# RMSNorm with SiLU on one core: block 0 loaded as two partition halves, one from each hardware queue

## The chip, the cores and the metric

The kernel runs on one core of a Trainium2 chip. The metric is device time in microseconds (us) of one execution. "Ratio" is always the mean time of one kernel's fast runs over the mean of the other kernel's fast runs of the same rounds on the same chip; it is therefore not exactly the ratio of the medians that stand beside it.

## The reference

```python
# x: 8 x 1024 x 2048 float32, gamma: 2048 float32, eps = 1e-5
rms = np.sqrt(np.mean(x ** 2, axis=-1, keepdims=True) + eps)
out = gamma * x / rms
return out * (1 / (1 + np.exp(-out)))
```

That is 8192 independent rows of 8 KB. 67.1 MB are read and 67.1 MB are written.

## The kernel before

The rows are cut into 16 blocks of 4 MB. A block is one tile of 128 partitions, and each partition holds 4 rows next to each other (32 KB). Six buffers go round. Loads are issued by SyncE (SP), stores and gamma by ScalarE (ACT).

```python
J = 4; BUFS, LEAD = 6, 6; nblk = n // (P * J)          # P = 128, nblk = 16
xb = x2.rearrange("(b p j) d -> b p (j d)", p=P, j=J)
...
def load(b):
    xt = pool.tile([P, J * d], f32, name="xt")
    nc.sync.dma_start(out=xt, in_=xb[b])
    blocks[b] = xt
...
def sums(b, after_first=()):
    ...   # sums of squares: two rows per partition on VectorE, two on ScalarE
    ...   # after ScalarE's first square: store(s) for the blocks in after_first
def store(b):
    nc.scalar.dma_start(out=ob[b], in_=blocks[b])
    if b + LEAD < nblk:
        load(b + LEAD)                                  # into the buffer just stored
...
grow = pool.tile([P, J * d], f32, name="xt")            # the sixth buffer takes gamma first
for b in range(BUFS - 1):
    load(b)
...
nc.scalar.dma_start(out=grow[0:P:P // Q, 0:w], in_=...) # gamma, 8 KB
...                                                     # TensorE spreads gamma over partitions
nc.vector.tensor_copy(out=g, in_=junk_v)                # stands before the first sums on VectorE
load(BUFS - 1)
...
for b in range(1, last - 1):
    sums(b + 1, after_first=[b - 1])
    finish(b)                                           # x * rstd * gamma, then SiLU
    invert(b + 1)
```

## Time and profile before

| | before |
|---|---|
| median time | 317.37 us (317.27 to 317.58), 3 runs |
| busy share of VectorE / ScalarE | 71% / 71% |
| load queue q1 plus store queue q10, share of 16 transfer engines | 98.9% |
| block 0 usable / first store issued | 13.2 us / 36.67 us |

The prediction below quotes the slice rows and the opening of this profile. Two more views of it matter later. The first is the page's row of rates, GB/s in 40 slices of 7.9 us:

```profile
GB/s 328 402 464 410 452 390 410 452 419 443 439 424 452 411 452 410 452 414 456 406 456 414 448 414 448 439 423 452 414 452 410 452 414 456 406 456 410 452 407 269
```

From the second slice to the last but one, the rate stands near 430 (390 to 464). The second view is busy time by stretches. Its last two columns are the share of the transfer engines (DMA) and GB/s. Both count a packet (here one partition's 32 KB), with all its time and bytes, in the stretch in which it starts, so a share can pass 1.

```profile
4.00:20.00 16.00, 2.09 (x8) 0.55 (x8) 7.28 (x7) 5.91 (x7) 0.00 (x0) 1.00 0.99 429
20.00:24.00 4.00, 0.00 (x0) 0.00 (x0) 4.00 (x2) 0.96 (x1) 0.00 (x0) 1.00 0.93 401
```

At 4 to 20 us a DMA share of 0.99 goes with 429 GB/s. A share and a rate say different things: the share says how long packets were in flight, the rate how much they carried. In this kernel they go together. Keep that pair for the comparison.

### The profile page before, as it was taken

The numbers are of one execution on the slowest core, as the hardware profiler recorded it, in microseconds if no ns is written. First come the engines' busy times: TensorE is split into PE (matmuls) and PEld (weight loads), VectorE is DVE, ScalarE is ACT, GpSimd is POOL, SyncE is SP. The second block draws the span as 40 slices with busy tenths as digits, with TensorE's granted clock in tenths as the row PEclk, the third lists the DMA queues.
The fourth block names the chain that finished last, engine by engine and source line by source line (L and its number), as shares of the span: only waits on it lengthen the run. The fifth ranks groups of instructions, "written<-read, shape, count | busy, mean of one in ns | idle before, by whom it ended". The sixth has DMA issues, their size and how long they took to land.

```text
span 316.3 us, 444 instructions
## 1 busy us (share of the span) xinstructions
PE 2.1 (1%) x8; PEld 0.5 (0%) x8; DVE 223.5 (71%) x147; ACT 223.8 (71%) x144; POOL 0.2 (0%) x4
## 2 busy tenths in 40 slices
PE   0200000000000000000000000000000000000000
PEld 0000000000000000000000000000000000000000
DVE  0679499999493983939849397593966939993900
ACT  1357958999967777678676687676786776879540
POOL 0000000000000000000000000000000000000000
DMA  8999999999999999999999999999999999999996
GB/s 328 402 464 410 452 390 410 452 419 443 439 424 452 411 452 410 452 414 456 406 456 414 448 414 448 439 423 452 414 452 410 452 414 456 406 456 410 452 407 269
DMA packets 4763, 134.25 MB, mean 425 GB/s; under 512 B 532, under 2 KB 532, under 8 KB 536
## 3 DMA queue, kind: packets, MB, share of 16 engines
q1 hardware_dynamic: 2304, 67.11, 49.7%
q10 hardware_dynamic: 2456, 67.12, 49.2%
q14 instruction: 3, 0.02, 0.0%
HBM read 67.12 MB, written 67.11 MB: 424 GB/s over the span
## 4 chain that ended last, share of the span: by engine, by line
DMA 74%; DVE 14%; ACT 5%; issue 2%; DVEq 1%; ACTq 0%; SPq 0%
DMA xt<-in_x_dram 44%; DMA out_dram<-xt 30%; DVE xt L84 11%; ACT xt L88 3%; DVE junk_v L64 3%; ACT junk_a L68 1%; DVEq L164 1%; ACT L74 0%; ACT rms L74 0%; DVE rstd L79 0%; ACTq L93 0%; DVE ss L64 0%; SPq L52 0%; DVEq L64 0%; ACTq L74 0%
## 5 line engine op out<-in xcount | busy, mean ns | idle before, releaser
L84 DVE SCALAR_TENSOR_TENSOR xt<-xt,rstd,g 128x2048 f32<-128x2048 f32 x64 | 146.2, 2347 | 0.1
L88 ACT ACTIVATE xt<-xt 128x4096 f32<-128x4096 f32 x32 | 115.4, 3615 | 36.8 <-DVE xt L84 36.7
L64 DVE CUSTOM_DVE_ANT_0 junk_v<-xt 128x2048 f32<-128x2048 f32 x32 | 73.5, 2298 | 56.1 <-DMA xt<-in_x_dram 55.5
L68 ACT ACTIVATE junk_a<-xt 128x2048 f32<-128x2048 f32 x32 | 60.1, 1879 | 29.2 <-DMA xt<-in_x_dram 28.3
L74 ACT ACT_TABLE_LOAD x15 | 19.2, 1283 | 9.9 <-DVE ss L64 9.9
L88 ACT ACT_TABLE_LOAD x15 | 19.2, 1283 | 3.1 <-DVE xt L84 2.9
L79 DVE RECIPROCAL rstd<-rms 128x4 f32<-128x4 f32 x16 | 2.8, 172 | 11.3 <-ACT rms L74 11.3
L114 DVE COPY g<-junk_v 128x2048 f32<-128x2048 f32 x1 | 2.3, 2292 | 9.2 <-PE junk_v L112 9.2
L68 ACT ACTIVATION_READ_ACCUMULATOR junk_a<-xt 128x1 f32 x32 | 6.0, 186 | 0.0
L74 ACT ACTIVATE rms<-ss,eps_t 128x4 f32<-128x4 f32 x16 | 4.8, 297 | 1.2 <-DVE ss L64 1.1
L64 DVE DVE_READ_ACCUMULATOR2_ANT ss<- 128x1 f32 x32 | 4.5, 141 | 0.0
L112 PE MATMUL junk_v<-xt,ones 1*128 1x512 f32 x8 | 2.1, 1133 | 8.1 <-DMA xt<-in_gamma_dram 8.1
L107 ACT ACT_TABLE_LOAD x1 | 1.3, 1283 | 0.7 <-PEq L150 0.7
L105 DVE MEMSET ones<- 128x128 f32 x1 | 0.2, 165 | 0.8 <-PEq L150 0.8
L112 PEld LDWEIGHTS junk_v<-xt,ones 1*128 1x128 f32 x8 | 0.5, 306 | 8.1 <-issue 8.1
L107 ACT ACTIVATE junk_a<-ones 128x1 f32<-128x1 f32 x1 | 0.2, 174 | 0.0
L150 POOL MEMSET const-uint8-127<- 128x1 uint8 x1 | 0.1, 102 | 0.0
L150 POOL MEMSET const-bfloat16-1.0<- 128x1 bf16 x1 | 0.1, 101 | 0.0
L150 POOL MEMSET const-float32-0.0<- 128x1 f32 x1 | 0.1, 98 | 0.2 <-issue 0.2
L150 POOL MEMSET const-float32-1.0<- 128x1 f32 x1 | 0.1, 98 | 0.0
L106 DVE MEMSET eps_t<- 128x1 f32 x1 | 0.1, 59 | 0.0
## 6 DMA issues: line engine op xcount, KB each, us to landing
xt<-in_x_dram SPq DMA_DIRECT2D x16, 4096.0 KB, 42.0
out_dram<-xt ACTq DMA_DIRECT2D x15, 4096.0 KB, 35.2
out_dram<-xt ACTq DMA_DIRECT2D x2, 2048.0 KB, 10.4
xt<-in_gamma_dram ACTq DMA_DIRECT2D x1, 8.0 KB
```

The costliest lines, as they stand in the source:

```text
L64: nc.vector.tensor_tensor_reduce(out=junk_v, in0=row(b, j), in1=row(b, j), scale=1.0, scalar=0.0, op0=ALU.mult, op1=ALU.add, accum_out=ss[ ...
L68: nc.scalar.activation(out=junk_a, in_=row(b, j), func=ACT.Square, accum_out=ss[:, j:j + 1])
L74: nc.scalar.activation(out=rms, in_=ss, func=ACT.Sqrt, scale=1.0 / d, bias=eps_t)
L79: nc.vector.reciprocal(out=rstd, in_=rmss.pop(b))
L84: nc.vector.scalar_tensor_tensor(out=row(b, j), in0=row(b, j), scalar=rstds[b][:, j:j + 1], in1=g, op0=ALU.mult, op1=ALU.mult)
L88: nc.scalar.activation(out=blocks[b][:, cols], in_=blocks[b][:, cols], func=ACT.Silu)
L105: nc.vector.memset(ones, 1.0)
L107: nc.scalar.activation(out=junk_a[:, 0:1], in_=ones[:, 0:1], func=ACT.Square)
L112: nc.tensor.matmul(junk_v[:, c * w:(c + 1) * w], ones[k:k + 1, :], grow[k:k + 1, 0:w], start=True, stop=True)
L114: nc.vector.tensor_copy(out=g, in_=junk_v)
L150: nc = _bacc.Bacc("TRN2", target_bir_lowering=False, num_devices=1)
L164: with _tile.TileContext(nc) as tc:
```

## The change

The intent is to have both hardware queues fetch block 0 at the start, where ScalarE's queue has nothing else to do. Here is the diff without an empty line:

```diff
     def load(b):
         xt = pool.tile([P, J * d], f32, name="xt")
-        nc.sync.dma_start(out=xt, in_=xb[b])
+        if b == 0:
+            nc.sync.dma_start(out=xt[0:P // 2, :], in_=xb[b][0:P // 2])
+            nc.scalar.dma_start(out=xt[P // 2:P, :], in_=xb[b][P // 2:P])
+        else:
+            nc.sync.dma_start(out=xt, in_=xb[b])
         blocks[b] = xt
```

## The prediction

> **What bounds the kernel now.** I read the page's slice rows and its queue table first[...]:
>
> ```profile
> DVE  0679499999493983939849397593966939993900
> ACT  1357958999967777678676687676786776879540
> DMA  8999999999999999999999999999999999999996
> ...
> q1 hardware_dynamic: 2304, 67.11, 49.7%
> q10 hardware_dynamic: 2456, 67.12, 49.2%
> ```
>
> The transfer engines are busy in all 40 slices, VectorE (DVE) and ScalarE (ACT) only 71% of the span each. q1 carries the loads, q10 the stores and gamma; together they fill 98.9% of 16 engines' time. 134.25 MB in 316.3 us is 424 GB/s. To see that this holds in each stage I asked for busy time in stretches; the last two columns are the share of the transfer engines and GB/s:
>
> ```profile
> 0.00:2.00 2.00, 0.00 (x0) 0.00 (x0) 0.17 (x2) 1.27 (x1) 0.20 (x4) 1.00 0.71 180
> 2.00:4.00 2.00, 0.00 (x0) 0.00 (x0) 0.00 (x0) 0.18 (x2) 0.00 (x0) 1.00 0.81 311
> ...
> 50.00:100.00 50.00, 0.00 (x0) 0.00 (x0) 43.40 (x29) 45.22 (x29) 0.00 (x0) 1.00 1.00 431
> 100.00:200.00 100.00, 0.00 (x0) 0.00 (x0) 69.00 (x45) 71.92 (x46) 0.00 (x0) 1.00 1.01 435
> ```
>
> From 4 us to the end nothing is idle. The list of who waited for whom agrees: VectorE's longest wait is for loads (55.5 us in 11 waits), and the store queue is never empty after the first store: a 4 MB store takes 35.2 us from issue to landing, where 4.19 MB at 431 GB/s is 9.7 us. So time lost by the transfer engines adds to the end, and time lost by VectorE or ScalarE doesn't, up to a slack. At the tail that slack is the last half store: issued at 304.77 us, landing after about 10.4 us, though 2.1 MB at 431 GB/s needs 4.9; some 5 us of other stores lay ahead of it. The opening, in order of time:
>
> ```profile
> 0.73 9.82 SPq L52 DMA_DIRECT2D xt<-in_x_dram  x6
> ...
> 1.03 1.09 ACTq L108 DMA_DIRECT2D xt<-in_gamma_dram  x1
> ...
> 8.09 2.09 PE L112 MATMUL junk_v<-xt,ones 1*128 1x512 f32 x8 [8.09 <-DMA xt<-in_gamma_dram]
> 10.24 2.29 DVE L114 COPY g<-junk_v 128x2048 f32<-128x2048 f32 x1 [9.24 <-PE junk_v L112]
> 13.19 1.88 ACT L68 ACTIVATE junk_a<-xt 128x2048 f32<-128x2048 f32 x1 [10.99 <-DMA xt<-in_x_dram]
> 13.24 2.30 DVE L64 CUSTOM_DVE_ANT_0 junk_v<-xt 128x2048 f32<-128x2048 f32 x1 [0.71 <-DMA xt<-in_x_dram]
> ```
>
> Block 0 lands at 13.1 us, and the copy of gamma is finished 0.7 us earlier. In the trace's packet records block 0 is eight 32 KB packets on each of 16 engines; the first took 1.55 to 2.28 us, the rest 1.21 to 1.23. I call 1.22 us a round. Gamma's four 2 KB packets, issued by 2.12 us, started only at 6.12, after three rounds of block 0, and their semaphore writes came one round later.
>
> [...] No run yet shows halves; that one queue alone fills the engines is shown (431 GB/s from 4.19 MB in 9.7 us, eight rounds of 1.22). [...] The trace agrees with a delay: gamma entered behind three committed packets. The first store agrees too: 24.75 us from issue to landing is about 8 own + 8 load + 4 committed rounds, 20 x 1.22 = 24.4. [...]
>
> **The change part by part.**
>
> *Removed and added.* SyncE's first 4 MB issue becomes a 2 MB issue, ScalarE gets a 2 MB issue ahead of its first table load. ScalarE's own cost is one issue, 0.34 (stores) to 1.09 us (gamma), while it waits 10.99 us for block 0 anyway: nothing. Bytes are the same; 16 more semaphore packets of 9 ns: nothing. SyncE's issues took 0.33 to 0.51 us each and are far ahead of the data: nothing.
>
> *Moved: block 0.* Half A (q1) and half B (q10) together are the same eight rounds, but q1 goes straight on with block 1. If B enters behind three committed packets, as gamma did, an engine's order is A A A B A B L B L B (L is block 1), and B ends in round 10 instead of 8. That is 2 x 1.22 = 2.4 us later: block 0 usable at 15.5, or 16.7 if its semaphore write waits another round. If both halves alternate from the start it stays at 13.1.
>
> *Moved: gamma.* It is now behind B on q10. Data at about 16, semaphore a round later (17.4), 0.45 us to PE as before: 17.9. Then 2.1 us PE and 2.3 us copy: VectorE reaches its first sum at 22.4 instead of 13.24, some 9 us late (6.5 if the halves alternate). VectorE is nearly solid from 28.96 to 79.5, so the first stores go out 6.5 to 9 us late, from 36.67 to 43 or 46.
>
> *Does that lateness reach the end?* The six loads need 48 rounds, until about 61 us, alone. A store issued at 46 meets 12 rounds of loads still to go; the other queue covers every gap, and store 1 (55.8 + 9 = 65) is out before store 0 lands (46 + 24.4 = 70). VectorE needs 4 x 2.35 + 2 x 2.30 + about 0.5 = 14.5 us per block against 19.5 of transfer (8.4 MB at 431), so it gains 5 us per block once loads pace it; it already waits 4.46 us at 84.1 and 5.54 at 103.5. Gone by block 7. Worth 0 on the end.
>
> [...] Four A packets and four B packets on each engine, all doubled because the engines run nearly in step (starts in a round spread over 0.6 us), cost 8 x 1.22 = 9.8 us. If engines fall out of step after the first three A packets [...], it is 3 x 1.22 = 3.7 us. The transfer engines have no idle time to give this back: it adds to the end, 321 to 327 us. Gamma and block 0 would come up to 12 us later still (first stores near 57 us), and by the same counting the queues only just stay fed; I allow 1 us for that.
>
> The sum: 317.4 + 0 (issues) + 0 (late gamma) + 0, 3.7 or 9.8 (ports) = 317.4, 321.1 or 327.2.
>
> **The rivals.** *It is hidden:* the engines are the limit and any order of the same packets ends together: 317.4. For it: mixed loads and stores also give 1.22 us a packet per engine, so the engine itself is a limit. [...] *Faster start:* two queues fill sooner. The first 4 us moved 0.98 MB, where 431 GB/s gives 1.72; that is 1.7 us lost, mostly the wait before 1.73 us and the first packet's 0.8 us of extra latency. Perhaps 0.3 us of it could be saved, so over 2% (6.3 us) faster is not to be had. *VectorE becomes the bound at the start:* the lateness above; it costs only if both queues run dry, which I counted against.
>
> **Range and chances.** [...] No effect is 30%, at 317.4 within 0.5. The distribution has two heaps; its middle is about 322. The range from 317.0 to 328.5 takes in both. Faster by over 2%: 2%, for a misread opening. Within 2%: 52%. Slower: 46%.
>
> **What would show it.** [...] rates in the first 25 us well under 431 (200 to 300 GB/s), first sums of block 0 at 20 to 30 us, and after 40 us the same 431 to 435 as before. Right for the hidden version: 431 GB/s from 4 us on, block 0's squares at 13 to 17 us, the gamma matmul at 15 to 18, first store at 43 to 46, and the same end. The step "lateness is worth 0" is wrong if a stretch after 40 us moves clearly less than 431 GB/s. The prediction is wrong altogether if a half uses fewer engines than 16, if the tail's 5 us slack is used up, or if the order of stores and loads changes for the rest of the run.

The 3.7 and 9.8 us that its sum calls ports were my estimate of what is lost if a packet of a half takes two rounds of 1.22 us instead of one, for three packets or for all eight; the trace of the kernel before has no load of half the partitions, and so shows no such packet. I gave some such effect 70%, and 46% to one above the 6.35 us that make 2%. That half a block is still spread over 16 engines was assumed too. Packets it calls committed are those that went ahead of a later issue: three rounds before gamma. That the queues take turns is in the packet records of the kernel before: the first store was issued at 36.67 us, its first packet started at 40.8, and from 44 to 57 us rounds of load and store packets alternate.

## The result, and the profile after

| | before | after |
|---|---|---|
| median time, 6 runs each | 317.48 us (317.27 to 317.81) | 326.60 us (326.38 to 326.76) |
| ratio | | 1.0287 (95%: 1.0274 to 1.0300) |
| span of the profiled run | 316.3 us | 324.9 us |

The change makes the kernel 9.1 us slower. The rows of the page after, and its queue table:

```profile
DVE  0004794999999999939397593957949399939100
ACT  1004369589999999996786676686676677795400
DMA  8999999999999999999999999999999999999996
GB/s 194 202 254 449 452 399 440 452 416 424 452 432 412 446 448 412 432 448 420 432 444 444 416 432 448 420 428 444 448 412 436 444 420 432 440 448 417 432 422 297
...
q10 hardware_dynamic: 2536, 69.22, 50.9%
q1 hardware_dynamic: 2240, 65.01, 48.0%
```

The DMA row is the same, digit for digit, as before. The GB/s row isn't: the first three of its slices (8.1 us each) carry a little over half of what they did. The stretches show the same:

```profile
4.00:20.00 16.00, 0.00 (x0) 0.00 (x0) 0.00 (x0) 0.00 (x0) 0.00 (x0) 1.00 1.07 229
20.00:24.00 4.00, 0.00 (x0) 0.00 (x0) 0.00 (x0) 0.00 (x0) 0.00 (x0) 1.00 0.74 262
24.00:50.00 26.00, 2.09 (x8) 0.55 (x8) 19.64 (x13) 13.80 (x9) 0.00 (x0) 1.00 1.00 429
50.00:100.00 50.00, 0.00 (x0) 0.00 (x0) 45.31 (x33) 44.92 (x33) 0.00 (x0) 1.00 1.01 438
100.00:200.00 100.00, 0.00 (x0) 0.00 (x0) 79.77 (x52) 85.28 (x55) 0.00 (x0) 1.00 1.00 430
```

From 4 to 20 us the transfer engines are as busy as before (1.07 against 0.99) but move 229 GB/s instead of 429. From 24 us on the rates are those of the kernel before. So the loss is one event, at the load of block 0. The packet records agree: counted at equal bytes moved, the changed kernel is 9.1 us behind at 4.5 MB and 8.7 to 10.0 us behind from 9 MB to the end, with no further loss.

The opening in order of time:

```profile
0.73 0.54 SPq L53 DMA_DIRECT2D xt<-in_x_dram  x1
0.73 0.58 ACTq L54 DMA_DIRECT2D xt<-in_x_dram  x1
...
1.41 1.14 ACTq L113 DMA_DIRECT2D xt<-in_gamma_dram  x1
...
24.13 1.88 ACT L72 ACTIVATE junk_a<-xt 128x2048 f32<-128x2048 f32 x1 [21.32 <-DMA xt<-in_x_dram]
...
26.37 2.09 PE L117 MATMUL junk_v<-xt,ones 1*128 1x512 f32 x8 [26.37 <-DMA xt<-in_gamma_dram]
...
28.52 2.29 DVE L119 COPY g<-junk_v 128x2048 f32<-128x2048 f32 x1 [27.52 <-PE junk_v L117]
30.85 2.30 DVE L68 CUSTOM_DVE_ANT_0 junk_v<-xt 128x2048 f32<-128x2048 f32 x1
```

Block 0 becomes usable at 24.13 instead of 13.19 us. Gamma follows on the store queue, and VectorE's first sum starts at 30.85 instead of 13.24 us. The first store goes out at 54.27 us, 17.6 later than before.

The packet records of the two traces give the size. Block 0 is 128 packets of 32 KB, eight on each of 16 engines (the records name the queue and not the engine; the rounds are read from the start times, which fall into eight groups of 16). All packets of block 0, the slow first round included, took 1.31 us on average before and 2.41 after: 8 x (2.41 - 1.31) = 8.8 us. The first packets of block 1 start at 12.40 us on average before and at 21.62 after, 9.2 us later: the 8.8, and 0.46 us by which the very first packets started later (2.38 us on average instead of 1.92). That is, within noise, the 9.1 us of the result (8.6 between the spans of the two profiled runs, of which the one before was slower than its median). The engines went through the rounds in step, in the order A A B A B A B B (A is the half of SyncE's queue, B the other): in each round all 16 packets are of the same half.

One view misleads here, the chain that ended last, by engine:

```profile
DMA 30%; ACT 19%; DVE 18%; another core or an unknown queue 18%; issue 7%; DVEq 1%; PE 1%; SPq 0%; ACTq 0%
```

Before, this chain was 74% DMA. Now it runs back through VectorE and ScalarE to the late gamma. Taken at its word it says that compute, and gamma, hold the end. Whether that is so is one of the questions for the experiments.

### The profile page after: what moved, and what is told of

It reads as the page before. It is cut to its first block, busy times and chain, and to the rows that moved or that the text cites. A ratio compares the mean times of both kernels' runs of the same rounds, so it can differ in the third digit from the quotient of the medians.

```text
span 324.9 us, 445 instructions
## 1 busy us (share of the span) xinstructions
PE 2.1 (1%) x8; PEld 0.5 (0%) x8; DVE 223.2 (69%) x147; ACT 223.2 (69%) x144; POOL 0.2 (0%) x4
## 4 chain that ended last, share of the span: by engine, by line
DMA 30%; ACT 19%; DVE 18%; another core or an unknown queue 18%; issue 7%; DVEq 1%; PE 1%; SPq 0%; ACTq 0%
DMA out_dram<-xt 14%; DVE xt L88 13%; ACT xt L92 13%; DMA xt<-in_x_dram 8%; DMA xt<-in_gamma_dram 8%; DVE junk_v L68 4%; ACT junk_a L72 2%; ACT L78 2%; ACT L92 2%; DVE g L119 1%; DVEq L169 1%; PE junk_v L117 1%; ACT rms L78 1%; SPq L56 0%
```

## The experiments

My theory: the packets of a transfer that covers only a contiguous range of the partitions slow each other, so that each takes two rounds instead of one. What slows them is shown by no run; that a packet takes two rounds in quarters and four in eighths, as the expectations below have it, was my estimate. In most of the expectations the first figure is the theory's and the last a rival's. The rivals are that two queues taking turns cost the time, that each cut of a transfer costs, that the order in which HBM is read costs, or that the late gamma and the late first store cost. Eleven kernels were run. All gave the right result except the two that are marked. Median of the kernel before: 317.86 us for same_queue, all_ports, late_gamma and mid_block, 317.57 for quarters, eighths, even_odd and store_halves, 317.64 for the other three.

### Both halves on one queue: same_queue

```diff
-            nc.scalar.dma_start(out=xt[P // 2:P, :], in_=xb[b][P // 2:P])
+            nc.sync.dma_start(out=xt[P // 2:P, :], in_=xb[b][P // 2:P])
```

> Both halves of block 0 go out on the load queue, none on the store queue. [...] 326.6 us as in the changed kernel, +9.1 over before; block 0's packets still about 2.4 us each, squares of block 0 at 22 to 24 us, gamma early again (PE at 8 to 12 us). Rival, that two queues taking turns on the load side cost the time: 317.5 us, packets 1.22 us each.

Measured: 327.40 us, ratio 1.0299 (1.0283 to 1.0314). The packets of block 0 took 2.53 us on average. The first square started at 23.97 us, gamma reached TensorE at 13.39. The second queue isn't the cause. VectorE's first sum started at 24.03 us, 6.8 us sooner than in the changed kernel, and the time was no better: a first hint that compute's lateness isn't what costs.

### The same halves of HBM spread over all partitions: all_ports

```diff
+        if b == 0:
+            src = x2[0:P * J].rearrange("(h p j) d -> h p (j d)", h=2, p=P)
+            nc.sync.dma_start(out=xt[:, 0:2 * d], in_=src[0])
+            nc.scalar.dma_start(out=xt[:, 2 * d:4 * d], in_=src[1])
...                                            # other blocks whole, as before
```

(The store of block 0 mirrors this layout.)

> Block 0 is again two 2 MB transfers from two queues, reading the same two halves of HBM in the same order, but each is spread over all 128 partitions (16 KB packets); its store mirrors this, so the result is right. [...] no loss, 317.5 us within 0.7; packets 0.6 us per 16 KB after the first; block 0 usable at 13 to 17 us. Rivals, that two queues, two halves or the HBM side of the halves cost the time: 326 us, or packets of 1.2 us per 16 KB.

Measured: 318.29 us, ratio 1.0014 (0.9999 to 1.0029), the same. After the first round the median 16 KB packet took 0.61 us, and block 0 was usable at 12.91 us. So two queues, two transfers and the two halves of HBM were harmless together where each transfer covered all partitions. The packets are half as long here, which the 2 x 2 test below avoids.

### Quarters and eighths: quarters, eighths

```diff
+        if b == 0:
+            step = P // 4                      # eighths: P // 8
+            for k in range(0, P, step):
+                nc.sync.dma_start(out=xt[k:k + step, :], in_=xb[b][k:k + step])
...                                            # other blocks whole, as before
```

> Block 0 as four transfers of 32 partitions on the load queue. [...] packets 2.4 us, 327.4 us as with both halves on one queue (+9.5). Rival, that the cost comes with each cut (per transfer): twice the cuts and more, 337 us or above.

> Block 0 as eight transfers of 16 partitions on the load queue. [...] packets 4.85 us, eight rounds of 4.85 for 1.22, +29 us, 347 us. Rival, that a cut block is read at half speed for another reason: 327 us.

Measured: quarters 327.05 us, ratio 1.0300 (1.0285 to 1.0316); eighths 343.12 us, ratio 1.0803 (1.0785 to 1.0821). The stretch from 4 to 20 us, quarters first, then eighths:

```profile
4.00:20.00 16.00, 1.54 (x8) 0.54 (x8) 0.00 (x0) 0.00 (x0) 0.00 (x0) 1.00 1.09 224
```

```profile
4.00:20.00 16.00, 0.00 (x0) 0.00 (x0) 0.00 (x0) 0.00 (x0) 0.00 (x0) 1.00 1.16 131
```

Four cuts cost what two cost (median packet 2.57 us, 224 GB/s), so it isn't a price per cut. With transfers of 16 partitions the stretch shows 131 GB/s, which flatters them, because a round that starts in it counts whole: 16 packets of 32 KB every 4.6 us are 114 GB/s (218 for the changed kernel's 2.4 us). The median packet took 4.61 us, 3.8 times the 1.21 of a whole block. So a packet took about 2, 2 and 4 rounds for halves, quarters and eighths (2.40, 2.57 and 4.61 us). The eighths cost 25.6 us, less than the 29 expected: a packet took 4.61, not 4.85, and the first round only 3.7 us, where the first round of a whole block takes 2.0 anyway. In the records, 8 x (4.50 - 1.31) = 25.5 us.

### Even and odd partitions: even_odd

```diff
-            nc.sync.dma_start(out=xt[0:P // 2, :], in_=xb[b][0:P // 2])
-            nc.scalar.dma_start(out=xt[P // 2:P, :], in_=xb[b][P // 2:P])
+            nc.sync.dma_start(out=xt[0:P:2, :], in_=xb[b][0:P:2])
+            nc.scalar.dma_start(out=xt[1:P:2, :], in_=xb[b][1:P:2])
```

> Block 0 as even partitions from the load queue and odd ones from the store queue[...]. [...] no loss, 317.7 us. If [...] an engine takes four neighbouring rows of the 64 in turn (partitions 8e, 8e+2, 8e+4, 8e+6)[...]: packets 2.4 us, 326.8 us. I hold the second for likelier (60%).

Measured: 317.61 us, ratio 1.0003 (0.9988 to 1.0018). The same stretch:

```profile
4.00:20.00 16.00, 2.09 (x8) 0.54 (x8) 1.07 (x1) 4.00 (x4) 0.00 (x0) 1.00 1.02 439
```

The whole loss is gone, with the same two queues, the same two transfers of 64 partitions and the same 32 KB packets (median 1.21 us). I had held the other outcome for likelier, at 60%. It rested on assumptions of mine about which rows an engine takes, in which order, and when engines slow each other; no run shows them, and the result contradicts what followed from them (326.8 us expected, 317.61 measured). Which of them fails, and which rows an engine takes, stays open. What the run shows is that halves of every second partition didn't collide.

The run shows a second thing. Its gamma is about as far behind as in the prediction's hidden version, so its compute starts late, while no transfer is slow. The first sum on VectorE and the first store:

```profile
21.25 2.30 DVE L68 CUSTOM_DVE_ANT_0 junk_v<-xt 128x2048 f32<-128x2048 f32 x1
...
44.67 0.36 ACTq L97 DMA_DIRECT2D out_dram<-xt  x1
```

Both are 8.0 us later than in the kernel before (13.24 and 36.67), and the end is the same.

### Which side, HBM or partitions: hbm_interleaved, sbuf_interleaved

Even_odd changed both sides of the transfer at once. These two change one side each, against the changed kernel. Block 0 comes out with its rows permuted. Their outputs are wrong, which doesn't matter for the times.

```diff
 # hbm_interleaved
-            nc.sync.dma_start(out=xt[0:P // 2, :], in_=xb[b][0:P // 2])
-            nc.scalar.dma_start(out=xt[P // 2:P, :], in_=xb[b][P // 2:P])
+            nc.sync.dma_start(out=xt[0:P // 2, :], in_=xb[b][0:P:2])
+            nc.scalar.dma_start(out=xt[P // 2:P, :], in_=xb[b][1:P:2])
 # sbuf_interleaved
+            nc.sync.dma_start(out=xt[0:P:2, :], in_=xb[b][0:P // 2])
+            nc.scalar.dma_start(out=xt[1:P:2, :], in_=xb[b][P // 2:P])
```

> The changed kernel with the HBM side alone interleaved: partitions 0 to 63 take the even 32 KB rows of block 0, partitions 64 to 127 the odd ones (block 0's rows come out permuted, a wrong result on purpose). [...] still 326.6 us, packets 2.4 us. If the way HBM is read decides (as the run with even and odd partitions, 317.6, would also allow): 317.6 us, packets 1.22 us.

> The changed kernel with the partition side alone interleaved: even partitions take the first 64 rows of block 0, odd ones the other 64 (a wrong result on purpose). [...] 317.6 us, packets 1.22 us. If the way HBM is read decides: 326.6 us.

Measured, with the changed kernel and even_odd as the other two corners:

| | HBM rows in halves | HBM rows interleaved |
|---|---|---|
| partitions in halves | 326.60 us, packets 2.40 us, ratio 1.0287 | 326.48 us, packets 2.38 us, ratio 1.0281 |
| partitions interleaved | 318.32 us, packets 1.21 us, ratio 1.0017 | 317.61 us, packets 1.21 us, ratio 1.0003 |

(Packets: median of block 0 after its first round.) The stretch from 4 to 20 us, hbm_interleaved and then sbuf_interleaved:

```profile
4.00:20.00 16.00, 0.00 (x0) 0.00 (x0) 0.00 (x0) 0.00 (x0) 0.00 (x0) 1.00 1.04 225
```

```profile
4.00:20.00 16.00, 2.09 (x8) 0.54 (x8) 0.60 (x1) 4.01 (x4) 0.00 (x0) 1.00 1.00 433
```

Only the partition side mattered here. How HBM was read made no clear difference (326.48 against 326.60 us, 317.61 against 318.32).

### How much lateness of the compute is free: late_gamma, gamma_behind_one

```diff
         for b in range(BUFS - 1):
             load(b)
+            if b == 1:                         # gamma_behind_one: b == 0
+                nc.sync.dma_start(out=grow[0:P:P // Q, 0:w], in_=...)   # gamma
...
-        nc.scalar.dma_start(out=grow[0:P:P // Q, 0:w], in_=...)
```

> The kernel before, with gamma's 8 KB issued on the load queue behind blocks 0 and 1, so that it lands at about 23 us and VectorE starts its sums near 28 us instead of 13.24; no transfer is slower. If lateness of the compute is worth 0 (theory): 317.5 us within 0.5, the first store at about 52 us. Rival, that the changed kernel loses part of its 9.1 us by its first store going out 17.6 us late: 320 to 326 us.

> The kernel before with gamma on the load queue behind block 0 alone: it lands near 13.5 us, VectorE's first sum at about 18 us, 5 us late where the run with gamma behind two blocks was 14 us late and lost 1.6 us. If only a lateness that lets the load queue run dry costs time: 317.6 us within 0.5 and no gap in the load queue. Rival, cost in proportion to the lateness: +0.6 us, 318.2.

Measured: late_gamma 319.47 us, ratio 1.0051 (1.0036 to 1.0066; under 2%, but clear of noise), first sum on VectorE at 27.38 us; gamma_behind_one 317.61 us, ratio 0.9997 (0.9982 to 1.0012), first sum at 17.59 us. A delay of 4.4 us is free, one of 14.1 us costs 1.6 us. My expectation of 0 for late_gamma failed. Busy time from 70 to 80 us in the kernel before, then in late_gamma:

```profile
70.00:80.00 10.00, 0.00 (x0) 0.00 (x0) 9.66 (x7) 9.91 (x8) 0.00 (x0) 1.00 1.00 433
```

```profile
70.00:80.00 10.00, 0.00 (x0) 0.00 (x0) 10.00 (x8) 9.91 (x8) 0.00 (x0) 1.00 0.95 370
```

The load queue started no data packet from 66.4 to 76.7 us, because it waited for the first store (issued at 50.80 us; the next load was issued at 72.30). The store queue kept the engines busy through that, but around the change-over packets were slower, up to 2.5 us instead of 1.21 for some. Summed over 70 to 90 us this is about 1.8 us per engine. Why they were slower there stays open. All_ports had a pause of 8.3 us on its load queue, with about 0.4 us of slower packets per engine, and showed no clear loss.

The changed kernel's first sum was 17.6 us late, yet its transfers were 9.2 us late too, so relative to them its compute was only about 8.4 us late. After 25 us its load packets never started more than 3.2 us apart (2.4 in the kernel before), and it lost nothing more to the end. Even_odd, with the same two issues and its compute 8.0 us late, lost nothing either. So the late gamma cost the changed kernel nothing that these runs show, in spite of the chain.

### In mid run, and for a store: mid_block, store_halves

```diff
 # mid_block, in load(b)
+        if b == 8:
+            nc.sync.dma_start(out=xt[0:P // 2, :], in_=xb[b][0:P // 2])
+            nc.sync.dma_start(out=xt[P // 2:P, :], in_=xb[b][P // 2:P])
...                                            # other blocks whole, as before
 # store_halves, in store(b)
+        if b == 8:
+            nc.scalar.dma_start(out=ob[b][0:P // 2], in_=blocks[b][0:P // 2])
+            nc.scalar.dma_start(out=ob[b][P // 2:P], in_=blocks[b][P // 2:P])
...                                            # other blocks whole, as before
```

> The kernel before, with block 8 (in mid run, stores interleaved) loaded as two partition halves on the load queue; block 0 is whole. [...] 8 more rounds, +9 us, 326.5 us; if store packets between them set the engines out of step, less: +3 to +9. Rival, that halves only cost at the cold start: 317.5 us.

> The kernel before with the store of block 8 as two partition halves on the store queue; every load is whole. [...] store packets of block 8 about 1.6 to 2.4 us, +6 to +9 us, about 325 us, as with block 8's load. Rival[...]: 317.7 us.

Measured: mid_block 325.60 us (324.19 to 326.35), ratio 1.0251 (1.0233 to 1.0269); store_halves 322.51 us, ratio 1.0158 (1.0143 to 1.0174; under 2%, but clear of noise). The stretch in which block 8 is loaded, before and then mid_block:

```profile
120.00:150.00 30.00, 0.00 (x0) 0.00 (x0) 20.92 (x15) 21.62 (x17) 0.00 (x0) 1.00 1.00 434
```

```profile
120.00:150.00 30.00, 0.00 (x0) 0.00 (x0) 13.80 (x9) 15.51 (x10) 0.00 (x0) 1.00 1.00 346
```

The cost is not one of the cold start. Amid stores it is 7.7 us instead of the 9.5 of same_queue, which is the same pair of transfers at the start. (The profiled run is the fastest of the four, 6.3 us over.) Block 8's own packets took 1.83 us on average, between one round and two. That engines fall out of step there, as the expectation guessed, is not shown.

A store by halves costs too, where the rival foretold nothing: 4.9 us, less than the 6 to 9 expected. The stretch in which block 8 is stored, before and then store_halves:

```profile
200.00:220.00 20.00, 0.00 (x0) 0.00 (x0) 13.80 (x9) 14.10 (x9) 0.00 (x0) 1.00 0.99 426
```

```profile
200.00:220.00 20.00, 0.00 (x0) 0.00 (x0) 13.80 (x9) 14.10 (x9) 0.00 (x0) 1.00 1.00 365
```

Most of the time is lost in this stretch (365 instead of 426 GB/s for 20 us is about 2.9 us), but the packet forecast missed: block 8's store packets took 1.43 us on average and 1.21 in the median (2.67 at most), not 1.6 to 2.4, and load packets beside them rose to about 1.4. So this store by halves cost time; what collides there is not shown.

## Why the prediction was wrong

- **What bounds the kernel** was right: transfers, in every stage. Time that the engines lost at the start (9.2 us at the start of block 1) reached the end whole within noise (9.1 us).
- **The issues, the moved bytes and the extra semaphore packets** were rightly put at nothing. Even_odd has all of them and ran at 317.61 us.
- **The step that failed is the term that the sum calls ports,** my estimate for packets of a half that slow each other. Its largest size was right: 8 x 1.22 = 9.8 us, 327.2 us in the sum; 8.8 us and 326.60 us were measured (less than 9.8 because the first round, 2.0 us long anyway, grew by only 0.2). But I gave it 0, 3.7 or 9.8 us, and from that mixture named about 322 us and "within 2%" as the likelier class (52%). So the term was mis-sized: hedged to some 4.6 us where 8.8 were lost. The runs put the full term in its place: 2.41 us per packet on average, in all eight rounds. The outcome "engines fall out of step", 3.7 us, did not happen: it needed the slowing to end after the first three packets of A, and in every round all 16 packets were of the same half and slow together (2.20 us on average in the first round, 2.39 to 2.57 in the others). That one of the named outcomes came true is no more than the hedge. The 30% for "no effect" had no run with halves behind it; 218 GB/s were measured for halves here (16 packets of 32 KB every 2.4 us).
- **That the partition side counts, and not something else about halves,** is shown by the 2 x 2 table: packets of 2.38 and 2.40 us with the partitions in halves, 1.21 with them interleaved. What collides in the hardware is not shown; the runs show only which sets of partitions do: contiguous 64, 32 and 16 (2.40, 2.57 and 4.61 us per packet), not every second one (1.21) and not all 128 (1.21).
- **The order of packets** was wrong in detail: A A A B A B L B L B was foretold, A A B A B A B B came. So B ended in round 8, not 10, and the engines went through A and B together, their starts in a round within about 1 us. Gamma entered behind three rounds in the kernel before, half B behind two in the changed one; what sets that number is not shown.
- **The hidden version** was right where the collision was taken away: even_odd had block 0's first square at 14.47 us (13 to 17 foretold), the gamma matmul at 16.78 (15 to 18), the first store at 44.67 (43 to 46) and the same end.
- **"Lateness is worth 0"** held for the changed kernel and for delays of 4.4 and 8.0 us. As a general step it is too broad: at 14.1 us the load queue ran dry and 1.6 us were lost. One reading on the way was off: VectorE isn't nearly solid from 28.96 to 79.5 us, it waits 4.56 us before 38.27; the conclusion didn't need it.
- **"Block 0's first sums at 20 to 30 us"** was nearly right: ScalarE began at 24.13, VectorE at 30.85, held by gamma. The rates from 4 to 24 us, 229 and 262 GB/s, lay in the forecast band.

## What to carry to other kernels

Where transfers are the bound, judge a transfer by the bytes per busy microsecond in its stretch, not by the busy share, which read 1.07 while the rate had halved (229 GB/s instead of 429). Loading a tile by contiguous halves of the partitions about halved the rate for that tile at the start, from one queue (224 GB/s) or two (229); in mid run it cost a little less (7.7 us), and a store by halves 4.9 us. If a split is needed, let each part reach all partitions (as in all_ports, 318.29 us) or take every second partition (even_odd, 317.61 us), which cost nothing clear here. No split version beat the kernel before, whose engines were full already (429 GB/s from 4 to 20 us).
